# The choice of experts without GpSimd: the shift moves behind the gather, the embedding's lows move to VectorE

## Chip, cores and metric

The kernel runs on 1 core of a Trainium2 chip. The metric is the device time of one execution in microseconds (us), the median of several runs.

## The reference

Two transformer blocks follow one another on 512 tokens of 1024 channels. The first one is what matters here: two layers, each a mixer (pooling and attention in layer 0, a state space model in layer 1) and then a mixture of experts. The second block adds, in each of its two layers, a gated projection of a per-token embedding `p`.

```python
h2 = modulate(rmsnorm(x, norm2_w[layer]), shift2, scale2)     # h * (1 + scale) + shift
ffn = hier_moe(h2, ...)
x = x + gate2[:, None, :] * ffn

def hier_moe(h, w_group, b_group, w_expert, b_expert, w1, w3, w2):
    g_prob = softmax(tf @ w_group + b_group)          # 4 groups, one is taken
    g_val, g_idx = lax.top_k(g_prob, 1)
    e_logits = einsum('td,dge->tge', tf, w_expert) + b_expert
    e_val, e_idx = lax.top_k(softmax(e_logits of that group), 2)   # 2 of its 8 experts
    ...
    hid = silu(t @ w1[e]) * (t @ w3[e])               # 32 experts of width 128
    y = sum over the two experts of weight * (hid @ w2[e])

# second block, each of two layers
x = x + sigmoid(rms_norm(x) @ ple_w_gate[i]) * (p[i] @ ple_w_proj[i])
```

All of it is computed to the accuracy of float32.

## The kernel before

The five engines are TensorE (PE, products into PSUM), VectorE (DVE), ScalarE (ACT), GpSimd (POOL) and SyncE (SP, which issues DMAs). Activations lie as eight tiles of 128 channels by 512 tokens (`xs`). To keep accuracy a large product is made of three: each operand is split into a `hi` in a rounded format (a copy on ACT) and a `lo`, the difference (a subtraction, the "low"); `split` (L220) does this, `wload` (L236) loads weights and splits them, and `lin` (L253) issues the three products L268, L269 and L270 for each 128 channels.

The place of the change is the passage between a layer's mixer and its experts, in `moe` (L721), once for each of the two layers:

- `moe_begin` and its `feed` bring the router's logits: for each of the eight channel tiles an ACT copy with the scale (L715) and a product with the router's weights (L717), issued among the mixer's last projections.
- `sumsq` (L372) and `newton` (L324 to L331) make the norm's rate of each token; `lT` and the product with `fold` (L750) turn the logits so that tokens lie on partitions; L768 and L770 complete them.
- `row(i)` makes the normed rows of 128 tokens, tokens on partitions: products of `xs` with the diagonal matrix `diag` of scales (L761), built by POOL at L736, copied from PSUM by ACT with the rate (L763); POOL adds `shift` (L764), a row spread over the partitions by products with the identity (L741) and two ACT copies (L743); SP stores the rows in DRAM, `srows` (L765).
- Some 24 short DVE operations choose group and experts (L780 to L811); `both` (L811) marks both experts of each token. PE counts (`cn` L815, `rp` L817 and L820), DVE turns counts into places (L823 to L834), masks `P` and `Q` (L859 to L868) give, by products (L876), for each place the token that stands there (`at`, L878). With it POOL issues eight indirect DMAs (L966) that fetch `srows` sorted by expert; PE turns each tile of 128 rows into channels (L972), and ACT and DVE copy them from PSUM to `hT` (L975, L977), halves of 512 columns each.
- The experts follow one by one: `begin(e)` loads 3 weight tiles of 512 KB and splits `hT`'s window (L928, L929), `halves` splits weights, `product` (L947), `gate`, `turned` and `second` do the rest.

The passage leaves PE free, so an independent piece of the second block is put there: `ple_proj` (L678), a generator that projects the embedding `p` of one layer in eight pieces of six products. Its input and first four weight tiles are split with the low on POOL (`eng=G`), its later weights with the low on DVE. `step(fill, 3)` issues three pieces ahead of the index products L876, `drain(fill)` the other five behind them; results go to DRAM (L695 by SP, L991 by POOL).

What sets the order: each engine runs its own list in order. A scheduler that works with estimated times makes these lists from the program, except for PE within `tc.manual_schedule`, where the written order holds. `tc.issue_after(x)` keeps an instruction behind `x` in that order; `ready` (the copy `lT`) and the entries of `later` are such marks. Buffers come from pools: `"w"` has 3 buffers, `"we"` 4, `"wh"` and `"wl"` 2 each, PSUM tags `"pa"` and `"pm"` 2 each.

Of the kernel before, what the change touches and what calls it, by code (L numbers as in the profile page):

```python
# [140 lines left out]
def _build(ctx, tc, A, out, dbg, upto, cap):  # L141
# [78 lines left out]
    def split(src, hi, lo, scale=None, eng=V):  # L220

        if scale is None:
            S.activation(hi, src, AF.Copy)  # L223
            eng.tensor_tensor(lo, src, hi.bitcast(F32), op=SUB)  # L224
        else:
            S.activation(hi, src, AF.Copy, scale=scale)
            return V.scalar_tensor_tensor(lo, src, scale, hi.bitcast(F32), op0=MUL, op1=SUB)
# [246 lines left out]
    def mod(l, seg, c):  # L474
        return mods[l][:, seg * 8 + c:seg * 8 + c + 1]
# [202 lines left out]
    def ple_proj(l, p, done, after, later):  # L678

        hi = tl(p, [128, 1024], "wh", 1, F32R)  # L680
        lo = tl(p, [128, 1024], "wl", 1, F32R)
        w = tl(wp, [128, 1024], "w", 3)
        nc.sync.dma_start(w.rearrange("p (k t) -> p k t", k=2), A["p"][l])
        with tc.issue_after(after):
            split(w, hi, lo, eng=G)
        acts = [(hi[:, k * T:(k + 1) * T], lo[:, k * T:(k + 1) * T]) for k in range(2)]
        for n in range(8):
            if n % 4 == 0:
                with tc.issue_after(later[0] if n else after):
                    wh, wl = wload(A[f"w_pp{l}"][n:n + 4].rearrange("n p k -> p n k"), 1024, 4, eng=V if n else G)  # L690
            first.append((wh[:, n % 4 * 256:(n % 4 + 1) * 256], wl[:, n % 4 * 256:(n % 4 + 1) * 256]))
            t = f_()
            S.activation(t, lin(A[f"w_pp{l}"][n], acts), AF.Copy, scale=0.5)
            if n < 4:
                nc.sync.dma_start(pp_d[l, n], t)  # L695
            else:
                done.append(t)
            yield
# [22 lines left out]
    def moe(l, mp, lp, br):  # L721
        with ExitStack() as st:
# [8 lines left out]
            hr = [hr[:, i * 1024:(i + 1) * 1024] for i in range(9)]  # L731
            yr = [yT[t // 4].rearrange("p c t -> p (c t)")[:, t % 4 * 1024:(t % 4 + 1) * 1024] for t in range(8)]

            diag, shift = hr[4].rearrange("p (c f) -> p c f", c=8), hr[5]
            o = slice(32, 40)
            G.tensor_tensor(diag, ident[:, None, :].to_broadcast([128, 8, 128]),  # L736
                            mods[l][:, o, None].to_broadcast([128, 8, 128]), op=MUL)
            for q in range(2):
                p = ps_("pa", 2)
                for c in range(4):  # L740
                    PE.matmul(p[:, c * 128:(c + 1) * 128], mod(l, 3, 4 * q + c).to_broadcast([128, 128]), ident,  # L741
                              start=True, stop=True)
                S.activation(shift[:, q * 512:(q + 1) * 512], p, AF.Copy)  # L743
            rate = rstd_of(sumsq(xs))

            lT = tl(ep, [128, T], "lT")
# [10 lines left out]
            def row(i):  # L757
                for q in range(2):
                    p = ps_("pm" if q else "pa", 2)
                    for c in range(4):  # L760
                        PE.matmul(p[:, c * 128:(c + 1) * 128], xs[4 * q + c][:, i * 128:(i + 1) * 128], diag[:, 4 * q + c],  # L761
                                  start=True, stop=True)
                    S.activation(hr[i][:, q * 512:(q + 1) * 512], p, AF.Copy, scale=rate[:, i:i + 1])  # L763
                G.tensor_tensor(hr[i], hr[i], shift, op=ADD)  # L764
                nc.sync.dma_start(srows[i * 128:(i + 1) * 128], hr[i])  # L765

            lg = tl(ep, [128, 4, 36], "lg")
# [2 lines left out]
            V.tensor_tensor(lg, lg, br[:, None, :].to_broadcast([128, 4, 36]), op=ADD)  # L770
            for i in range(4):
                row(i)

            def b3(a, n):
                return a[:, :, None].to_broadcast([128, 4, n])
# [32 lines left out]
                                o[:, :, None, :].to_broadcast([128, 4, 4, 8]), op=MUL)  # L808
                oh.append(e)
            both = tl(ep, [128, 4, 32], "both")  # L810
            V.tensor_tensor(both, oh[0], oh[1], op=ADD)  # L811

            cn = ps_("pa", 2)
            for i in range(4):
# [149 lines left out]
            for t in range(8):  # L964
                g = yr[t]
                last = G.indirect_dma_start(out=g, out_offset=None, in_=srows,  # L966
                                            in_offset=bass.IndirectOffsetOnAxis(ap=at[:, t:t + 1], axis=0),
                                            bounds_check=511, oob_is_err=False)
                for q in range(2):
                    p = ps_("pm" if q else "pa", 2)  # L970
                    for c in range(4):
                        PE.transpose(p[:, c * 128:(c + 1) * 128], g[:, (4 * q + c) * 128:(4 * q + c + 1) * 128], ident)  # L972
                    o, pv = hT[:, 4 * q:4 * q + 4, t * 128:(t + 1) * 128], p.rearrange("p (c f) -> p c f", c=4)
                    if q:
                        S.activation(o, pv, AF.Copy)  # L975
                    else:
                        V.tensor_copy(o, pv)  # L977
                if t == 3:
                    parts = [halves(w) for w in ws[:2]]
                if t == 0:  # L980
                    ws, v, hh, hl_ = begin(0, ws)
                if t == 7:
                    hp = ps_()
                    for n in range(2):
                        product(hp, n, hh, hl_, parts[n])
                    hd, mul = gate(hp)
                if t == 7:
                    second(ws[2], turned(hd), v)
# [1136 lines left out]
```

## Time and profile before

| what | us |
|---|---|
| median of 3 runs | 2476.03 |
| lowest and highest | 2470.3, 2476.96 |
| the profiled execution, its own time | 2467.97 |
| its span, first to last instruction | 2466.2 |
| PE busy | 2339.5 (95%) |
| DVE busy | 1764.8 (72%) |
| ACT busy | 1090.6 (44%) |
| POOL busy | 518.4 (21%) |

A matmul row counts as busy while its columns stream through the array, with a modelled end, so rows overlap by a little; a float32 product is two passes and counts twice. "PEclk" is the granted clock as a share of 2.4 GHz; the chip grants 1.2 or 2.4 GHz. An idle time stands in brackets with the instruction that ended it.

### The profile page before, as it was taken

The page shows a single profiled execution, that of the slowest core. Times are in us where ns is not written, and L with a number is a line of the kernel's source. Part 1 is how long each engine was busy: PE and PEld are TensorE (multiplying, and loading weights), DVE is VectorE, ACT ScalarE, POOL GpSimd, SP SyncE. Part 2 cuts the span into 40 slices and gives each one's busy share as a digit, 9 for nine tenths or more (in the row PEclk, how much of TensorE's full clock was granted, in tenths as well). Part 3 has the DMA queues.
Part 4 walks back from the last instruction along what each step waited for, and adds up shares of the span by engine and source line. Part 5 has one row for each costly group of instructions (what it writes and reads, how often), then busy time and mean ns, then how long its engine had stood idle before and what let it go on. Part 6 is the DMA issues. An engine that isn't in the chain of part 4 may idle for free.

```text
span 2466.2 us, 35818 instructions
## 1 busy us (share of the span) xinstructions
PE 2339.5 (95%) x13205; PEld 1921.3 (78%) x13206; DVE 1764.8 (72%) x3319; ACT 1090.6 (44%) x1706; POOL 518.4 (21%) x510
## 2 busy tenths in 40 slices
PE   7999899899999998999989999999999899999999
PEld 4767799677777775899766777778787788888887
DVE  6985678699996886667686677737847756745755
ACT  3444588434443434786334434324433234433432
POOL 0001444100000002444110295666520000000000
PEclk9999899899999998999899999999999899999999
DMA  9862699554345222897421233344337632323342
GB/s 347 291 207 82 234 324 331 170 181 128 117 140 180 86 70 100 295 329 251 138 69 61 83 105 119 102 132 123 98 113 239 204 111 94 100 86 106 97 125 94
DMA packets 136790, 385.95 MB, mean 156 GB/s; under 512 B 24696, under 2 KB 41208, under 8 KB 134560
## 3 DMA queue, kind: packets, MB, share of 16 engines
q1 hardware_dynamic: 121408, 338.51, 41.5%
q0 software_dynamic: 7552, 26.74, 3.1%
q10 hardware_dynamic: 7648, 18.32, 2.1%
q8 instruction: 109, 1.79, 0.3%
q14 instruction: 73, 0.60, 0.1%
HBM read 354.13 MB, written 29.38 MB: 156 GB/s over the span
## 4 chain that ended last, share of the span: by engine, by line
PE 43%; DVE 7%; ACT 1%; issue 1%; DMA 0%; ACTq 0%; DVEq 0%
PE ps L268 13%; PE ps L270 13%; PE ps L269 13%; DVE wl L224 1%; DVE hc L2013 1%; ACT wh L223 0%; DMA tab<-tab_d 0%; PE pm L372 0%; PE sk L1587 0%; PE pa L512 0%; PE pm L530 0%; PE ps L1091 0%; PE ps L1092 0%; PE po L538 0%; DVE hc L2017 0%
## 5 line engine op out<-in xcount | busy, mean ns | idle before, releaser
L268 PE MATMUL ps<-hi,wh 128*128 128x512 f32 (+2 forms) x2248 | 898.9, 400 | 3.9 <-ACT hi L485 3.2
L270 PE MATMUL ps<-hi,wl 128*128 128x512 f32 (+2 forms) x2248 | 884.6, 394 | 8.8 <-DVE wl L224 8.8
L269 PE MATMUL ps<-lo,wh 128*128 128x512 f32 (+2 forms) x2248 | 884.5, 394 | 3.1 <-DVE lo L486 2.4
L223 ACT ACTIVATE wh<-w 128x1024 fp32r<-128x1024 f32 (+2 forms) x327 | 310.8, 951 | 572.1 <-PE ps L269 376.6
L224 DVE TENSOR_TENSOR wl<-w,wh 128x1024 fp32r<-128x1024 f32 (+3 forms) x323 | 371.3, 1150 | 211.6 <-ACT wh L223 207.3
L270 PEld LDWEIGHTS ps<-hi,wl 128*128 128x128 f32 (+1 forms) x2248 | 424.4, 189 | 109.2 <-DVE wl L224 13.8
L268 PEld LDWEIGHTS ps<-hi,wh 128*128 128x128 f32 (+1 forms) x2248 | 425.5, 189 | 106.7 <-issue 12.4
L269 PEld LDWEIGHTS ps<-lo,wh 128*128 128x128 f32 (+1 forms) x2248 | 425.2, 189 | 96.2 <-DVE lo L486 4.3
L224 DVE TENSOR_TENSOR wl<-we,wh 128x1024 fp32r<-128x1024 f32 x128 | 169.4, 1336 | 61.1 <-ACT wh L223 59.1
L929 POOL TENSOR_TENSOR hl<-hT,hh 128x1024 fp32r<-128x1024 f32 x60 | 138.4, 2307 | 173.3 <-ACT hh L928 96.0
L2013 DVE SCALAR_TENSOR_TENSOR hc<-f,cols,hc 128x511 f32<-128x511 f32 (+1 forms) x176 | 152.4, 866 | 6.4 <-ACT hc L2011 3.2
L223 ACT ACTIVATE wh<-we 128x1024 fp32r<-128x1024 f32 x128 | 135.3, 1059 | 47.6 <-PE pa L947 23.3
L909 PE MATMUL ps<-ht,w 128*128 128x128 f32 x1024 | 125.9, 276 | 5.2 <-ACT ht L959 5.0
L909 PEld LDWEIGHTS ps<-ht,w 128*128 128x128 f32 x1024 | 119.4, 192 | 7.4 <-ACT ht L959 7.1
L726 POOL IOTA io<- 128x512 f32 x2 | 1.1, 562 | 572.0 <-PE ps L270 415.6
L2009 DVE TENSOR_TENSOR f<-ps,rb 128x512 f32<-128x512 f32 x88 | 60.4, 686 | 71.2 <-PE ps L270 70.9
L441 DVE CUSTOM_DVE_ANT_0 we<-we,crow 128x1024 f32<-128x1024 f32 x80 | 96.3, 1214 | 3.4 <-DMA we<-in_ada_t_dram 3.1
L947 PE MATMUL pa<-wh,hh 128*128 128x256 f32 x496 | 89.2, 301 | 0.0
L223 ACT ACTIVATE hi<-hc 128x512 fp32r<-128x512 f32 x44 | 27.8, 632 | 128.0 <-DVE hc L2017 128.0
L491 DVE SCALAR_TENSOR_TENSOR x<-ps,mod,x 128x512 f32<-128x512 f32 x52 | 38.9, 748 | 59.0 <-PE ps L270 51.5
L947 PE MATMUL pa<-wl,hh 128*128 128x256 f32 x496 | 78.7, 281 | 1.4 <-DVE wl L224 1.4
L947 PE MATMUL pa<-wh,hl 128*128 128x256 f32 x496 | 79.1, 281 | 0.0
(572 smaller groups left out, 3319.1 us busy)
## 6 DMA issues: line engine op xcount, KB each, us to landing
we<-in_w_ex_dram SPq DMA_DIRECT2D x128, 512.0 KB, 5.7
w<-in_w_fu_dram SPq DMA_DIRECT2D x88, 512.0 KB, 3.5
we<-in_ada_t_dram SPq DMA_DIRECT2D x80, 512.0 KB, 5.0
w<-in_w_ex_dram SPq DMA_DIRECT2D x64, 512.0 KB, 5.4
w<-in_w_si_dram SPq DMA_DIRECT2D x48, 512.0 KB, 3.5
w<-in_w_fd_dram SPq DMA_DIRECT2D x32, 512.0 KB, 3.8
w<-in_w_ei_dram SPq DMA_DIRECT2D x20, 512.0 KB, 3.6
aw<-in_ada_w_dram SPq DMA_DIRECT2D x16, 512.0 KB, 10.2
```

The costliest lines, as they stand in the source:

```text
L223: S.activation(hi, src, AF.Copy)
L224: eng.tensor_tensor(lo, src, hi.bitcast(F32), op=SUB)
L268: PE.matmul(ps[:m], a, h, start=(not more and k + j == 0), stop=False)
L269: PE.matmul(ps[:m], a, l, start=False, stop=False)
L270: PE.matmul(ps[:m], b, h, start=False, stop=(last and k + j == nk - 1))
L441: V.tensor_tensor_reduce(w, w, row, 1.0, 0.0, op0=MUL, op1=ADD, accum_out=st[:, n:n + 1])
L491: V.scalar_tensor_tensor(xs[c], ps, mod(l, seg, c), xs[c], op0=MUL, op1=ADD)
L909: PE.matmul(p[:, c * 128:(c + 1) * 128], w2[:, (4 * q + c) * 128:(4 * q + c + 1) * 128], hd, start=True, stop=True)
L929: (V if e < 2 else G).tensor_tensor(hl_, win, hh.bitcast(F32), op=SUB)
L947: PE.matmul(hp[:, 0:256], h[:, 4 * n + k], w[:, k * 256:(k + 1) * 256], start=(n + i + k == 0), stop=(n + i + k == 6))
L2009: V.tensor_tensor(t, next(up)[1], rb, op=MUL)
L2013: V.scalar_tensor_tensor(c[:, d:], t[:, :T - d], C(f"fw{l}{2 - d}", n), c[:, d:], op0=MUL, op1=ADD)
```

## The change

The shift row is no longer made, and no row gets it before it is stored. It is added where the gathered and turned rows leave PSUM: there channels lie on partitions, so that the shift is one number a partition; DVE's copy becomes an addition, ACT's copy of four channel groups becomes four activations with a bias. In `ple_proj` the input and the first weights get their `hi` on ACT right behind `ready`, and their lows on DVE, behind `both` (which is now the first entry of `later`); the first part of the generator is issued by `step(fill)` ahead of the choice.

```diff
@@ ple_proj
+        wq = tl(wp, [128, 1024], "w", 3)
+        nc.sync.dma_start(wq.rearrange("p (a k) -> p a k", a=4), A[f"w_pp{l}"][0:4].rearrange("n p k -> p n k"))
+        wh, wl = (tl(wp, [128, 1024], g, 2, F32R) for g in ("wh", "wl"))
         with tc.issue_after(after):
-            split(w, hi, lo, eng=G)
+            S.activation(hi, w, AF.Copy)
+            S.activation(wh, wq, AF.Copy)
+        yield
+        with tc.issue_after(later[0]):
+            V.tensor_tensor(lo, w, hi.bitcast(F32), op=SUB)
+            V.tensor_tensor(wl, wq, wh.bitcast(F32), op=SUB)
         acts = [(hi[:, k * T:(k + 1) * T], lo[:, k * T:(k + 1) * T]) for k in range(2)]
         for n in range(8):
-            if n % 4 == 0:
-                with tc.issue_after(later[0] if n else after):
-                    wh, wl = wload(A[f"w_pp{l}"][n:n + 4].rearrange("n p k -> p n k"), 1024, 4, eng=V if n else G)
+            if n == 4:
+                with tc.issue_after(later[1]):
+                    wh, wl = wload(A[f"w_pp{l}"][n:n + 4].rearrange("n p k -> p n k"), 1024, 4)
@@ moe
-            for q in range(2):
-                p = ps_("pa", 2)
-                for c in range(4):
-                    PE.matmul(p[:, c * 128:(c + 1) * 128], mod(l, 3, 4 * q + c).to_broadcast([128, 128]), ident,
-                              start=True, stop=True)
-                S.activation(shift[:, q * 512:(q + 1) * 512], p, AF.Copy)
@@ row(i)
-                G.tensor_tensor(hr[i], hr[i], shift, op=ADD)
@@ behind the four rows
+            step(fill)
@@ both
-            V.tensor_tensor(both, oh[0], oh[1], op=ADD)
+            later.append(V.tensor_tensor(both, oh[0], oh[1], op=ADD).ins)
@@ the gathered rows
                     if q:
-                        S.activation(o, pv, AF.Copy)
+                        for c in range(4):
+                            S.activation(o[:, c], pv[:, c], AF.Identity, bias=mod(l, 3, 4 + c))
                     else:
-                        V.tensor_copy(o, pv)
+                        V.tensor_tensor(o, pv, mods[l][:, 24:28, None].to_broadcast([128, 4, 128]), op=ADD)
```

How the lists of instructions move, at three places. The first is PE's list in layer 0, from the logits' column of the seventh channel tile to the fold; `f` is a scaled channel tile, `acc` the summed squares of seven tiles, and in the second L372 row `f` the squares of the eighth. Before:

```order
L717 MATMUL pm<-f,wr 64x512
L741 MATMUL pa<-ident,mod_127 128x128 x6
L717 MATMUL pm<-f,wr 64x512
L741 MATMUL pa<-ident,mod_127 128x128 x2
L372 MATMUL pm<-ones,acc 128x1 x4
L761 MATMUL pa<-hT,x_71 128x128
L761 MATMUL pa<-hT,x_73 128x128
L372 MATMUL pm<-ones,f 128x1 x4
L750 MATMUL pm<-fold,lT 128x36 x4
```

Now:

```order
L725 MATMUL pm<-f,wr 64x512
L372 MATMUL pm<-ones,acc 128x1 x4
L763 MATMUL pa<-hT,x_71 128x128
L372 MATMUL pm<-ones,f 128x1 x4
L763 MATMUL pa<-hT,x_73 128x128
L763 MATMUL pa<-hT,x_75 128x128
L725 MATMUL pm<-f,wr 64x512
L763 MATMUL pa<-hT,x_77 128x128
L752 MATMUL pm<-fold,lT 128x36 x4
```

The products of the shift row are gone, and both products of the sums of squares stand ahead of the last logits' column instead of behind it.

The second is DVE's list in layer 0 behind `both`. Before:

```order
L811 TENSOR_TENSOR both<-oh_2280,oh_2282 128x128 [waits DVE_49]
L849 SCALAR_TENSOR_TENSOR gs<-e2m,gs 128x4 [waits DVE_49,Activation_49]
L850 RECIPROCAL wt<-gs 128x4 [waits DVE_49]
L823 SCALAR_TENSOR_TENSOR off<-ones,pa 128x32 [waits PE_49]
L851 TENSOR_TENSOR wt<-wt,e2m 128x4 [waits DVE_49]
L824 TENSOR_TENSOR off<-off,pa 128x32 [waits DVE_49]
L840 TENSOR_REDUCE most<-pa 1x1
L838 TENSOR_SCALAR ow<-off 1x32 [waits DVE_49]
L826 TENSOR_TENSOR pl<-pa,off 128x128 [waits PE_49]
```

Now:

```order
L813 TENSOR_TENSOR both<-oh_2274,oh_2276 128x128 [waits DVE_49]
L692 TENSOR_TENSOR wl<-w,wh 128x1024 [waits DMAHW1_49]
L825 SCALAR_TENSOR_TENSOR off<-ones,pa 128x32 [waits PE_49]
L693 TENSOR_TENSOR wl<-w,wh 128x1024 [waits DMAHW2_49]
L826 TENSOR_TENSOR off<-off,pa 128x32 [waits DVE_49]
L842 TENSOR_REDUCE most<-pa 1x1
L828 TENSOR_TENSOR pl<-pa,off 128x128 [waits DVE_49,PE_49]
```

Two operations of 1024 elements a partition stand on either side of the scan of the counts (`off`, the row that waits for PE), and the three short ones on the experts' weights have moved further back.

The third is ACT's list in layer 0 at the last gathered tile. Before:

```order
L975 ACTIVATE hT<-pm 128x4x128 [waits PE_49] x4
L919 TENSOR_LOAD ow [waits DVE_49]
L928 ISA
L928 ACTIVATE hh<-hT 128x1024 [waits DVE_49,Activation_49]
L223 ACTIVATE wh<-we 128x1024 [waits PE_49]
L952 ACT_TABLE_LOAD
```

Now:

```order
L978 ACTIVATE hT<-pm,mod_127 128x128 [waits PE_49]
L978 ACTIVATE hT<-pm,mod_127 128x128 x3
L223 ACTIVATE wh<-we 128x1024 [waits PE_49]
L921 TENSOR_LOAD ow [waits DVE_49]
L930 ISA
L930 ACTIVATE hh<-hT 128x1024 [waits DVE_49,Activation_49]
L954 ACT_TABLE_LOAD
```

Each half tile is four activations instead of one, and a weight copy stands ahead of the second expert's activations `hh` instead of behind them; DVE's list changes in the same way. On SP's list one expert weight of the two that stood ahead of the stores of the rows (L765) now stands right behind them, the other behind two stores of `ple_proj`'s results.

## Rows read from the trace of the kernel before

**Rows 1.** Timeline of PE, both layers (start us, length us, instruction [idle before <- releaser]).

```profile
229.27 1.60 PE L741 MATMUL pa<-ident,mod 128*128 128x128 f32 x12
...
242.99 1.06 PE L761 MATMUL pm<-hT,x 128*128 128x128 f32 x8
...
252.02 1.89 PE L815 MATMUL pa<-both,ones 128*128 128x32 f32 x8 [6.19 <-DVE both L811]
...
977.09 1.89 PE L815 MATMUL pa<-both,ones 128*128 128x32 f32 x8 [10.53 <-DVE both L811]
```

**Rows 2.** Stretches: us, busy PE, PEld, DVE, ACT, POOL; PEclk, DMA share, GB/s.

```profile
236.00:241.00 5.00, 3.50 (x19) 3.31 (x17) 4.55 (x12) 0.27 (x1) 2.84 (x2) 0.70 0.53 140
...
255.40:259.40 4.00, 4.00 (x11) 3.15 (x11) 3.64 (x19) 0.60 (x1) 0.00 (x0) 0.50 0.21 83
...
272.00:287.00 15.00, 9.97 (x71) 9.14 (x71) 8.91 (x12) 6.55 (x11) 4.73 (x7) 0.89 0.89 355
```

**Rows 3.** Timeline of DVE, layer 0.

```profile
234.88 1.68 DVE L324 TENSOR_SCALAR rsi<-rsv 128x4 int32<-128x4 int32 x1
236.59 2.27 DVE L326 TENSOR_SCALAR rsy<-rsi 128x4 int32<-128x4 int32 x1
...
240.74 0.31 DVE L768 TENSOR_TENSOR lg<-pm,rsy 128x144 f32<-128x144 f32 x1
...
242.32 2.15 DVE L787 TENSOR_TENSOR go<-go,gk 128x16 f32<-128x16 f32 x1
244.50 2.39 DVE L795 TENSOR_TENSOR el<-lg,go 128x128 f32<-128x128 f32 x1
...
247.55 1.59 DVE L782 TENSOR_TENSOR e1o<-eg,e1m 128x32 f32<-128x32 f32 x1
```

**Rows 4.** Timeline of POOL, layer 0.

```profile
228.43 1.90 POOL L736 TENSOR_TENSOR hT<-ident,mod 128x1024 f32<-128x1024 f32 x1 [70.06 <-PE ps L270]
234.17 4.67 POOL L224 TENSOR_TENSOR wl<-w,wh 128x1024 fp32r<-128x1024 f32 x2 [3.85 <-ACT wh L223]
242.07 7.02 POOL L764 TENSOR_TENSOR hT<-hT 128x1024 f32<-128x1024 f32 x3 [3.23 <-ACT hT L763]
```

**Rows 5.** Timeline of DVE, layer 1: first and last of six long operations.

```profile
957.37 0.17 DVE L324 TENSOR_SCALAR rsi<-rsv 128x4 int32<-128x4 int32 x1
...
960.62 2.04 DVE L770 TENSOR_TENSOR lg<-lg,br 128x144 f32<-128x144 f32 x1
...
972.62 1.58 DVE L782 TENSOR_TENSOR e1o<-eg,e1m 128x32 f32<-128x32 f32 x1
```

**Rows 6.** Timeline of POOL: the first gather of layer 0 and of layer 1.

```profile
263.87 1.25 POOL L966 DMA_INDIRECT yT<-srows,at  x1 [3.24 <-DVE af L880]
...
988.26 1.05 POOL L966 DMA_INDIRECT yT<-srows,at  x1 [2.57 <-DVE af L880]
```

**Rows 7.** Timeline of PE: the first expert's first product in either layer.

```profile
286.07 1.03 PE L947 MATMUL ps<-wh,hh 128*128 128x256 f32 x4
...
1008.29 0.71 PE L947 MATMUL ps<-wh,hh 128*128 128x256 f32 x4
```

**Rows 8.** Timeline of DVE, layer 0: the offsets, and the low behind the masks.

```profile
255.65 0.29 DVE L826 TENSOR_TENSOR pl<-pa,off 128x128 f32<-128x128 f32 x1 [0.79 <-PE pa L820]
...
259.25 1.22 DVE L224 TENSOR_TENSOR wl<-w,wh 128x1024 fp32r<-128x1024 f32 x1
```

**Rows 9.** Timeline of PE, layer 0: first of 30 embedding products, and what follows them.

```profile
263.22 0.48 PE L268 MATMUL ps<-wh 128*128 128x512 f32 x1
...
270.30 1.85 PE L886 MATMUL pm<-Qw,hh 128*128 128x8 f32 x16
```

**Rows 10.** Copies from PSUM: two rows of ACT's timeline, one group of the page.

```profile
286.45 0.60 ACT L975 ACTIVATE hT<-pm 128x512 f32<-128x512 f32 x1 [1.11 <-PE pm L972]
...
291.61 0.27 ACT L959 ACTIVATE ht<-pm 128x128 f32<-128x128 f32 x1
...
L2009 DVE TENSOR_TENSOR f<-ps,rb 128x512 f32<-128x512 f32 x88 | 60.4, 686 | 71.2 <-PE ps L270 70.9
```

More of the change, by code (lines that the diff above doesn't have):

```diff
@@ L732, in moe @@
             yr = [yT[t // 4].rearrange("p c t -> p (c t)")[:, t % 4 * 1024:(t % 4 + 1) * 1024] for t in range(8)]
-            diag, shift = hr[4].rearrange("p (c f) -> p c f", c=8), hr[5]
+            diag = hr[4].rearrange("p (c f) -> p c f", c=8)
             o = slice(32, 40)
```

## The prediction

> **What bounds the kernel now.** TensorE (PE) is busy nearly all of the span, so time can be won only where it stands still or runs at its lower clock. I looked at the busy slices of the page first, then at tables of stretches and the timelines by engine, for the two places the diff touches: the choice of experts in layer 0 (about 229 to 291 us) and in layer 1 (953 to 1013 us). All times below are moments of that trace. Three things are to be seen.
>
> First, PE waits for VectorE (DVE). The counts of the tokens per expert (L815) start after 6.19 us of idle in layer 0 and 10.53 us in layer 1, both times released by `both` [rows 1]. Behind the wait PE stands at half clock: the granted clock is 0.50, that is 1.2 GHz instead of 2.4, while the first embedding products run [rows 2].
>
> Second, DVE is late because of GpSimd (POOL). Operations on 4 to 128 elements a partition last 1.59 to 2.39 us where their like last 0.16 to 0.31 [rows 3]. Each of the long ones ends within 0.15 us of the end of a POOL instruction: POOL runs two lows (L224) from 234.17 and three shift additions (L764) from 242.07, about 2.34 us each, so their ends fall at 236.5, 238.8, 244.4, 246.8 and 249.1 [rows 4]; L324 ends at 236.56, L326 at 238.86, L787 at 244.47, L795 at 246.89, L782 at 249.14. The same L324 takes 0.17 us in layer 1, where POOL starts its lows later; there L770, further on, takes 2.04 [rows 5]. So the excess is a wait for POOL, not work.
>
> Third, the stage behind, in which eight gathers fetch the rows and PE turns them, is set by transfers: from 272 to 287 us PE works 10 of 15 us and the DMA engines are busy 0.89 of the time at 355 GB/s [rows 2]. It starts with the first gather, at 263.87 and 988.26 [rows 6], and ends with the first expert's product, at 286.07 and 1008.29 [rows 7]: 22.2 and 20.0 us.
>
> **What the change does, part by part.**
>
> *POOL's six instructions of each layer go* (four shift additions, two lows). With them go the excesses. Layer 0, against 0.17, 0.17, 0.17, 0.30 and 0.19 us for their like: L324 1.51, L326 2.10, L787 1.98, L795 2.09, L782 1.40; 3.6 before the logits (L768), 5.5 behind them [rows 3]. Layer 1: six such operations from L770 to L782 of `e1o`, by the same subtraction 11.1 us, all behind the logits [rows 5]. From the logits (L768, in layer 1 just ahead of L770, at 960.27) to the release of the counts the chain then takes 252.02 - 240.74 - 5.5 = 5.8 us in layer 0 and 977.09 - 960.27 - 11.1 = 5.7 in layer 1.
>
> *The eight small products that made the shift row (L741) go, with their two copies on ACT.* In layer 0 they stood between the sums of squares and the last logit column: 1.60 us for twelve passes [rows 1], four more behind it. The order now has the sums ahead of that column. From the end of the last projection at 229.27: sums 0.8 us, one row product that waits for `diag` (L736 on POOL, done at 230.33 [rows 4]), sums 0.8, so L324 could start near 231.9 instead of 234.88 and its chain, eleven short operations of 0.2 each, would end near 234.3. PE does the last column, the copy of it and the fold, and the logits start at 234.9 instead of 240.74: 5.8 us earlier, the 3.6 of above in it. In layer 1 the fold bounds them; that gives 0.5 us, and ten of the sixteen passes stood earlier among the projections: 10 x 0.11 = 1.1 us.
>
> *Where `both` is early, PE's rows end last.* The chain alone would release the counts at 240.7 and 965.5. Behind the fold PE has seven row groups of eight passes, 1.06 us with 0.17 of it under the next [rows 1]: 6.2 us, to 240.9 and 965.8. The counts start at 241.0 and 965.9 instead of 252.02 and 977.09. Layer 0 shows a granted clock of 0.70 from 236 to 241 us [rows 2], right behind many one-column products, and those stay; I charge 1.8 us for it in layer 0 alone. So the counts gain 9.2 and 11.2 us.
>
> *The lows are now two VectorE operations right behind `both`* (1.22 us each, by the second weights' low of the same shape [rows 8]), with the scan of the counts between them. Behind the start of the counts: counts 0.9 at full clock, scan 0.2, second low 1.2, two short ones 0.3; the offsets (L826) start at +2.75. From there to the end of the masks is 3.6 us before [rows 8], 0.3 more now since three short operations of the weights have moved in: +6.6. PE: its 18 products cannot pass the third before the second low, then 16 at 0.236 us (30 of them lie between 263.22 and 270.30 [rows 9]): +6.3, so they are hidden. The index products take 1.85 and the hand-over 0.5: the gathers start at +8.95 where they started at +11.85 and +11.17. That is 2.9 and 2.2 us more, and only because PE, no longer idle, keeps its full clock. If it doesn't, 16 passes of 0.21 (L815, at half clock [rows 1]) and 18 products of up to twice 0.236 make it up to +14.2: a loss of 2.4 and 3.0.
>
> The Trainium skill, page Perfetto Trace Analysis, section Optimizing Scalar/DVE Operations, speaks against this part: where VectorE is saturated, move some of its work to ScalarE or even GpSimd. By that alone the sum would lose the four lows, 4.9 us, and win nothing, as in the slower rival below. The section goes on that the two share a read port of SBUF, so that moving work between them might not help; the trace sides with that half, since VectorE's long operations end with GpSimd's.
>
> *The shift is added when turned rows leave PSUM.* On DVE a copy becomes an addition of the same 128x512, 0.69 us by a like one (L2009) [rows 10]; the copies overlap the gathers: nothing. On ACT one copy of 0.60 becomes four of 128x128, between 0.6 in all and 4 x 0.27 = 1.1 [rows 10]; I take 1.1. Eight times that is 8.6 us in a stage of 20 to 22: hidden. Only the last tile's lies open: +0.5.
>
> *Behind it* the order has a weight copy and its low (1.05 and 1.2 us) ahead of the second expert's activations, where they stood behind. With +0.5 and +1.05 on ACT and 1.2 on DVE the second expert's activations come up to 2.8 us later, while PE has the first one's 24 products to do. Bounds of PE's wait: 0 and 2.8. I take the middle, 1.3 a layer.
>
> *SP's queue.* The buffers of the lows come free later, so two expert weights that were loaded ahead of the rows' stores now stand behind them, the second behind two stores of products. By my times it lands just before the gathers; if not, it delays them by 0.5 MB at 355 GB/s, 1.5 us. I take 0, and 1.5 into the range.
>
> **Sum.** Layer 0: 9.2 + 2.9 - 1.3 = 10.8. Layer 1: 11.2 + 1.1 + 2.2 - 1.3 = 13.2. Together 24.0 us. The profiled execution took 2467.97 us (span 2466.2), so 2444; the median of the runs shown stands 8 us higher, at 2476.0, which makes 2452.
>
> **The rivals.**
> - *Half clock.* PE's stretch of short products puts it at 1.2 GHz for the rows or the products of both layers. Rows then take about 6 us longer, or the products lose 5 us, as above. Some 6 us a layer instead of the charged 1.8 in one: 24 - 10 = 14, so 2462. For: 0.70 and 0.50 were granted here. Against: the long idle ahead of the counts goes.
> - *The gathers take it back.* If weights loads meet the gathers in both layers (1.5 each) and the second expert waits the full 2.8, 6 us go: 2458.
> - *Hidden anyway.* If the stream of expert weights set the experts' end by itself, an earlier start would be given back and only a little of the sum would stay, about 2474. Against: the stream's loads start when products free their buffers, so they move with PE.
> - *Slower.* The long operations are VectorE's own and not POOL's; then nothing shrinks, the four lows lie on its chain, and the second expert waits: 4 x 1.22 + 2 x 1.4 = 7.7, so 2484. It decides as soon as the excess stays above the lows, 2.4 us a layer. Against: the ends that coincide.
>
> **How the numbers follow.** Forecast 0.62, half clock 0.17, gathers 0.12, hidden 0.06, slower 0.03. The range runs from no charge for clock and second expert (24 + 1.8 + 2.6, and some us of scatter: 2444) to half clock with the gathers' loss (14 - 5 = 9: 2466). About 0.3% (7.4 us) is what a measurement can tell from no change: faster 0.88 (forecast, clock, gathers, less a little), same 0.08, slower 0.04.
>
> **What would show it.** DVE's operations between the sums and `both` all under 0.4 us; PE's idle ahead of the counts under 2 us; granted clock 1.00 over the first products; first gather 10 to 14 us earlier relative to the last projection; the stretch from gather to first product unchanged at 20 to 22 us. I am wrong if long operations remain, if the clock stays at 0.50, or if that last stretch grows by several us.

## The result, and the profile after

| | before | changed |
|---|---|---|
| median, us | 2475.84 (2470.30 to 2476.96) | 2451.95 (2448.66 to 2458.73) |
| ratio, with its 95% interval | 1 | 0.9895 (0.9875 to 0.9915) |
| the profiled execution: its time, and its span | 2467.97, 2466.2 | 2448.66, 2446.9 |
| granted clock, mean over the span | 0.973 | 0.979 |

The change makes the kernel faster, by 1.05% on the ratio and by 23.9 us, or 0.96%, between the medians in the table. The forecast was 2452.0. The two profiled executions lie closer together, 19.3 us apart by time and by span. Two more series of the changed kernel, each beside the kernel before on the same chip, gave 0.9862 (0.9845 to 0.9879) and 0.9890 (0.9867 to 0.9913), so the gain lies between 24 and 34 us by series. What follows are the places that the prediction spoke of. Line numbers of the changed kernel stand one to three above those of the kernel before, and eight above them between `ple_proj` and the place where the shift row was made (L717 is now L725).

DVE in layer 0, timeline of the changed kernel, in answer to [rows 3] and [rows 8]:

```profile
232.62 0.17 DVE L324 TENSOR_SCALAR rsi<-rsv 128x4 int32<-128x4 int32 x1
...
235.74 0.31 DVE L769 TENSOR_TENSOR lg<-pm,rsy 128x144 f32<-128x144 f32 x1 [0.99 <-PE pm L752]
...
237.32 0.17 DVE L789 TENSOR_TENSOR go<-go,gk 128x16 f32<-128x16 f32 x1
237.53 0.29 DVE L797 TENSOR_TENSOR el<-lg,go 128x128 f32<-128x128 f32 x1
...
241.37 1.22 DVE L692 TENSOR_TENSOR wl<-w,wh 128x1024 fp32r<-128x1024 f32 x1
```

The operations that took 1.59 to 2.39 us in layer 0 take 0.17 to 0.29. The wait that is left in this chain is one for PE's fold (0.99). The first low follows behind the sum of the masks.

PE, timeline of the changed kernel, in answer to [rows 1] and [rows 7]:

```profile
228.96 1.07 PE L725 MATMUL pm<-f,wr 128*64 128x512 f32 x2
...
240.98 1.06 PE L763 MATMUL pm<-hT,x 128*128 128x128 f32 x8
241.87 0.98 PE L817 MATMUL pa<-both,ones 128*128 128x32 f32 x8
...
271.80 0.71 PE L949 MATMUL ps<-wh,hh 128*128 128x256 f32 x4
...
275.35 0.74 PE L949 MATMUL pa<-wh,hh 128*128 128x256 f32 x4 [0.53 <-ACT hh L930]
276.80 0.74 PE L949 MATMUL pa<-wh,hl 128*128 128x256 f32 x4 [0.71 <-DVE hl L931]
...
940.40 1.07 PE L725 MATMUL pm<-f,wr 128*64 128x512 f32 x2
...
944.94 1.97 PE L725 MATMUL pm<-f,wr 128*64 128x512 f32 x2
...
954.84 0.98 PE L817 MATMUL pa<-both,ones 128*128 128x32 f32 x8
...
983.82 0.72 PE L949 MATMUL ps<-wh,hh 128*128 128x256 f32 x4
...
988.80 0.74 PE L949 MATMUL pa<-wh,hl 128*128 128x256 f32 x4 [0.71 <-DVE hl L931]
```

The counts (L817) follow the last row group without idle time in both layers, where 6.19 and 10.53 us stood. They take 0.98 us instead of 1.89: PE has its full clock. Two smaller waits are new, ahead of the second expert. In layer 1 the last logits' column (944.94) takes 1.97 us instead of 1.07; the granted clock of its stretch is in the next table.

Stretches of the changed kernel (us, busy time of PE, PEld, DVE, ACT, POOL; PEclk, DMA share, GB/s), in answer to [rows 2]:

```profile
240.00:250.00 10.00, 10.00 (x70) 8.82 (x69) 8.83 (x37) 4.75 (x10) 1.21 (x1) 1.00 0.82 283
...
260.00:271.80 11.80, 6.93 (x53) 5.51 (x53) 8.50 (x12) 8.78 (x29) 3.25 (x5) 1.00 0.90 363
941.00:946.00 5.00, 4.89 (x26) 3.40 (x24) 2.10 (x13) 1.24 (x2) 1.51 (x1) 0.76 0.00 0
```

Over the counts and the first products PE is busy all of the time at full clock. In the gather stage the DMA engines are still busy 0.90 of the time at 363 GB/s, and PE only 6.93 of 11.80 us. The trace now puts most of PE's waits there down to the evictions by ACT and DVE, 4.0 us in layer 0, so that the transfers alone set the stage isn't shown; it did not get longer. The clock was lost in another place: 0.76 over layer 1's logits.

POOL, timeline of the changed kernel: the first gathers, in answer to [rows 6].

```profile
250.46 1.25 POOL L968 DMA_INDIRECT yT<-srows,at  x1 [1.03 <-DVE af L882]
...
963.41 1.05 POOL L968 DMA_INDIRECT yT<-srows,at  x1 [1.01 <-DVE af L882]
```

They start 13.41 and 24.85 us earlier than before. By layer 1's second expert (its `hl` product, 1011.64 before, 988.80 now) the changed kernel leads by 22.8 us, close to the sum of 24.0; the choice of both layers lies ahead of that point. At the end of the span the lead is 19.3 us.

### The profile page after: what moved, and what is told of

Its sections match the earlier page's. It is cut to its first block, busy times and chain, and to the rows that moved or that the text cites. A ratio compares the mean times of both kernels' runs of the same rounds, so it can differ in the third digit from the quotient of the medians.

```text
span 2446.9 us, 35789 instructions
## 1 busy us (share of the span) xinstructions
PE 2328.9 (95%) x13173; PEld 1906.3 (78%) x13174; DVE 1750.3 (72%) x3323; ACT 1096.4 (45%) x1750; POOL 486.6 (20%) x498
## 4 chain that ended last, share of the span: by engine, by line
PE 43%; DVE 7%; ACT 1%; issue 1%; DMA 0%; SPq 0%; POOL 0%; ACTq 0%; DVEq 0%; POOLq 0%
PE ps L268 13%; PE ps L270 13%; PE ps L269 13%; DVE wl L224 2%; DVE hc L2016 1%; ACT wh L223 1%; PE pm L372 0%; PE sk L1590 0%; PE pa L512 0%; DMA w<-w_d 0%; PE pm L530 0%; PE py L1715 0%; PE po L538 0%; DVE hc L2020 0%; PE pm L1580 0%
## 5 line engine op out<-in xcount | busy, mean ns | idle before, releaser
L223 ACT ACTIVATE wh<-w 128x1024 fp32r<-128x1024 f32 (+3 forms) x323 | 306.9, 950 | 572.9 <-PE ps L269 384.6
L911 PE MATMUL ps<-ht,w 128*128 128x128 f32 x1024 | 125.7, 276 | 5.1 <-ACT ht L961 5.1
L911 PEld LDWEIGHTS ps<-ht,w 128*128 128x128 f32 x1024 | 119.4, 191 | 7.0 <-ACT ht L961 6.9
L949 PE MATMUL pa<-wh,hh 128*128 128x256 f32 x496 | 88.4, 300 | 1.0 <-ACT hh L930 1.0
L949 PE MATMUL pa<-wh,hl 128*128 128x256 f32 x496 | 78.8, 280 | 1.4 <-DVE hl L931 1.4
L949 PE MATMUL pa<-wl,hh 128*128 128x256 f32 x496 | 78.6, 280 | 0.0
```

Source lines behind the costliest of these rows:

```text
L911: PE.matmul(p[:, c * 128:(c + 1) * 128], w2[:, (4 * q + c) * 128:(4 * q + c + 1) * 128], hd, start=True, stop=True)
L949: PE.matmul(hp[:, 0:256], h[:, 4 * n + k], w[:, k * 256:(k + 1) * 256], start=(n + i + k == 0), stop=(n + i + k == 6))
```

## The experiments

All of them are judged by their ratio to the kernel before on the same chip. The theory was the forecast's: work on POOL makes DVE's small operations wait. Line numbers in rows are those of the kernel shown.

**1. The first lows back on POOL, the shift left behind the gather.**

```diff
             S.activation(hi, w, AF.Copy)
+            G.tensor_tensor(lo, w, hi.bitcast(F32), op=SUB)
             S.activation(wh, wq, AF.Copy)
+            G.tensor_tensor(wl, wq, wh.bitcast(F32), op=SUB)
...
-        with tc.issue_after(later[0]):
-            V.tensor_tensor(lo, w, hi.bitcast(F32), op=SUB)
-            V.tensor_tensor(wl, wq, wh.bitcast(F32), op=SUB)
```

> The embedding's first two low parts go back to GpSimd; everything else is as after the change. Theory (what GpSimd does beside VectorE stretches VectorE's long operations): one to three of the long ones of each layer come back (the logits' copy or additions at 2 us or more where the changed kernel has 0.17 to 0.3), 2 to 6 us more than after for both layers together, so 2454 to 2458 us, with no low part between the sum of the chosen (line 813) and the copy of the counts. Rival (VectorE is the one that was loaded, the lows cost it 1.2 us each on the way): this is up to 4.9 us faster than the changed kernel, 2447 to 2452 us, and the long operations stay short.

Measured: 2457.65 us, ratio 0.9918 (0.9894 to 0.9943). DVE has less to do than in the changed kernel, and the time is longer, as the theory had it (2454 to 2458). By the ratios alone that is weak, since the interval touches those of two of the changed kernel's three series (0.9895 and 0.9890); the trace is what shows it. Timelines of POOL and DVE, layer 0:

```profile
237.78 2.36 POOL L689 TENSOR_TENSOR wl<-w,wh 128x1024 fp32r<-128x1024 f32 x1 [4.58 <-ACT wh L688]
240.11 2.43 POOL L691 TENSOR_TENSOR wl<-w,wh 128x1024 fp32r<-128x1024 f32 x1
...
237.94 0.31 DVE L768 TENSOR_TENSOR lg<-pm,rsy 128x144 f32<-128x144 f32 x1 [0.99 <-PE pm L751]
238.28 2.03 DVE L770 TENSOR_TENSOR lg<-lg,br 128x144 f32<-128x144 f32 x1
240.34 0.17 DVE L781 TENSOR_REDUCE gm<-lg 128x4 f32<-128x16 f32 x1
240.55 2.02 DVE L783 TENSOR_TENSOR go<-lg,gm 128x16 f32<-128x16 f32 x1
```

POOL's lows end at 240.14 and 242.54, DVE's two long operations at 240.31 and 242.57. L768 has the same size as L770 and runs beside the same low in 0.31 us: one of its inputs is in PSUM, while both inputs of L770 are in SBUF. A reduction (one input) isn't held either. The counts then wait 3.13 us in layer 0 and 2.93 in layer 1, where the changed kernel has no wait. The theory holds; the rival, that the lows weigh on DVE, would have made this kernel the faster one. The advice weighed in the prediction, that moving work of a saturated VectorE to ScalarE or even GpSimd may make sense (the Trainium skill, page Perfetto Trace Analysis, section Optimizing Scalar/DVE Operations), wins nothing here, 0.9918 against the changed kernel's 0.9862 to 0.9895; the section's own doubt, that it might not help because the two share a read port, fits what this run's rows show.

**2. The shift back ahead of the stores, the lows left on DVE.** The row's products, its copies and POOL's four additions come back, with plain evictions behind the gather (the change's own lines in `moe`, undone).

> The shift row, its TensorE products and GpSimd's four additions per layer come back ahead of the stores of rows; the embedding's lows stay on VectorE. Theory (GpSimd's work stretches VectorE's): most of the change's gain goes, 12 to 18 us for both layers, so 2464 to 2470 us; the one-hot or threshold operations of layer 0 take 1.5 us or more again, and TensorE idles several us ahead of the count products. Rival (the order of TensorE's work alone, the shift's products ahead of the logits): 3 to 5 us more than after, 2455 to 2457 us, with the small VectorE operations at 0.2 to 0.3 us.

Measured: 2466.97 us, ratio 0.9951 (0.9934 to 0.9968), as the theory had it. By the ratios the shift alone would give about 0.8% (run 1) and the lows alone 0.5% (this run), 20 and 12 us of that chip's 2480. Timelines of POOL, DVE and PE, layer 0:

```profile
249.84 2.35 POOL L772 TENSOR_TENSOR hT<-hT 128x1024 f32<-128x1024 f32 x1 [2.66 <-ACT hT L771]
...
249.89 3.38 DVE L692 TENSOR_TENSOR wl<-w,wh 128x1024 fp32r<-128x1024 f32 x1
...
250.12 1.88 PE L824 MATMUL pa<-both,ones 128*128 128x32 f32 x8 [6.08 <-DVE both L820]
```

And a stretch of it:

```profile
250.00:255.00 5.00, 4.88 (x19) 4.27 (x20) 4.99 (x8) 0.00 (x0) 2.19 (x1) 0.50 0.26 105
```

DVE's low, 1.22 us long in the changed kernel, takes 3.38. It begins 0.05 us behind a POOL addition of 2.35 us, and what is left of that addition and 1.22 us of its own make up the 3.38 to within 0.15. PE's wait ahead of the counts is back, and behind it the granted clock of 0.50.

**3. POOL works, but nothing waits for it.** Four additions on POOL per layer whose result nobody reads; rows are stored as in the changed kernel, and PE's list is the changed kernel's.

```diff
                     S.activation(hr[i][:, q * 512:(q + 1) * 512], p, AF.Copy, scale=rate[:, i:i + 1])
+                G.tensor_tensor(hr[5], hr[i], hr[4], op=ADD)
                 nc.sync.dma_start(srows[i * 128:(i + 1) * 128], hr[i])
```

> The changed kernel with one more GpSimd addition behind each of the four gathered-row blocks of each layer (it reads two tiles in SBUF and writes one that nobody uses); no wait is added for any other engine. Theory: VectorE's small two-input operations that fall beside them take 1.5 us or more, TensorE runs out of fill ahead of the counts, and the time is 5 to 15 us above the changed kernel's, 2457 to 2467 us. Rival (GpSimd's additions cost only because the rows' stores waited for them): the time stays at 2450 to 2454 us.

Measured: 2468.72 us, ratio 0.9957 (0.9938 to 0.9976), 1.7 us above the expected stretch. POOL's and DVE's timelines, layer 0, and PE's:

```profile
239.30 9.62 POOL L766 TENSOR_TENSOR hT<-hT 128x1024 f32<-128x1024 f32 x4 [6.75 <-ACT hT L765]
...
240.03 1.66 DVE L785 TENSOR_TENSOR e1o<-eg,e1m 128x32 f32<-128x32 f32 x1
241.73 2.40 DVE L787 TENSOR_TENSOR e1o<-e1o,desc 128x32 f32<-128x32 f32 x1
244.16 0.19 DVE L789 TENSOR_REDUCE e1k<-e1o 128x4 f32<-128x32 f32 x1
244.39 2.17 DVE L790 TENSOR_TENSOR e1o<-e1o,e1k 128x32 f32<-128x32 f32 x1
246.59 2.38 DVE L804 SCALAR_TENSOR_TENSOR e<-e1o,eg 128x32 f32<-128x32 f32 x1
...
250.99 1.89 PE L818 MATMUL pa<-both,ones 128*128 128x32 f32 x8 [7.42 <-DVE both L814]
```

This is the cleanest of the runs. No engine waits for the additions' result, and still four operations of 32 elements a partition take 1.7 to 2.4 us, the counts wait 7.42 us (7.02 in layer 1), and about as much is lost as when the shift itself comes back (0.9957 against 0.9951). So the cost comes without any store that waits for POOL; the rival had put it there.

**4. POOL writes, but doesn't read.** Eight fills of a tile by POOL behind the diagonal. In layer 0 they run from 231.60 to 239.61 us, beside the rate, the logits and the choice of the group; run 3's additions came later, beside the choice of the experts (239.30 to 248.92).

```diff
+            for _ in range(8):
+                G.memset(hr[5], 0.0)
```

> The changed kernel with eight GpSimd fills of a tile (128x1024, write only) per layer behind the diagonal. If only GpSimd work that reads SBUF stretches VectorE's two-input operations, the logits' additions and one-hots stay at 0.17 to 0.5 us and the time within 2 us of the changed kernel, 2450 to 2454 us; the copies and threshold operations alone may stretch. If any GpSimd work does it, it looks like the run with additions: operations of 1.5 us or more and 2457 to 2467 us.

Measured: 2450.65 us, ratio 0.9880 (0.9852 to 0.9908), the changed kernel's. POOL's and DVE's timelines, layer 0:

```profile
231.60 8.01 POOL L747 MEMSET hT<- 128x1024 f32 x8
...
233.27 0.32 DVE L324 TENSOR_SCALAR rsi<-rsv 128x4 int32<-128x4 int32 x1
233.62 0.97 DVE L326 TENSOR_SCALAR rsy<-rsi 128x4 int32<-128x4 int32 x1
...
238.31 0.31 DVE L773 TENSOR_TENSOR lg<-lg,br 128x144 f32<-128x144 f32 x1
...
238.85 0.17 DVE L786 TENSOR_TENSOR go<-lg,gm 128x16 f32<-128x16 f32 x1
```

POOL is busy for 8 us, and of DVE's operations in that time only the two integer ones of the tensor-scalar form are held, until the fill then under way ends (8.01 us for eight, so about 1 us each). The two-input operations L773 and L786 keep their 0.31 and 0.17 us; beside the lows of run 1 the same two (L770 and L783 there) took 2.03 and 2.02. So two kinds of waiting stood in [rows 3]: L324 and L326 waited beside the lows there and wait beside the fills here, the two-input ones waited only beside POOL work that reads SBUF. The time of this run says less, since its fills lie elsewhere than run 3's additions.

The Trainium skill, page SBUF — State Buffer, section Who interferes with whom, gives this as its rule: DVE's second pair of SBUF ports is GpSimd's as well and is held by one of them for a whole instruction; a DVE operation with two inputs in SBUF collides with GpSimd instructions that read SBUF and not with those that only write, reductions never collide, and forms such as the tensor-scalar one can take the pair when they run in their fast mode. The waits of runs 1, 3 and 4 agree with each of these points, with the rows above; the ports themselves are in no row, and that L324 and L326 ran in such a mode is not shown by one either.

**5. The tail: is the new wait ahead of the second expert worth anything?** The second half of expert 1's weights is split behind that expert's `hh` and `hl` instead of ahead of them, in ACT's and DVE's lists. In run 6 the last gathered tile is also evicted by DVE alone.

```diff
-                    parts.append(halves(ws[1]))
+                    if e == 1:
+                        with tc.issue_after(behind[0]), tc.issue_after(behind[1]):
+                            parts.append(halves(ws[1]))
+                    else:
+                        parts.append(halves(ws[1]))
```

> The changed kernel itself, as the reference on this chip for the three that follow: 2446 to 2459 us, as in its first runs, and a ratio to before of 0.987 to 0.992.

> The changed kernel with the second half of expert 1's weights split behind that expert's input halves (lines 930 and 931) on ScalarE and VectorE, instead of ahead of them. Theory (the tail's 1.3 us per layer is this queue): TensorE's two waits ahead of the second expert (0.53 and 0.71 us in layer 0, 0.49 and 0.71 in layer 1) fall to 0.3 us in all or less, and the time is 1 to 2.5 us below the changed kernel's of the same chip. Rival (the gate of the first expert, now behind that split on ScalarE, is waited for instead): the waits move to the turned gate (line 959 there) and the time stays within 1 us.

> As the run before it, and the last gathered tile's second half is also evicted by VectorE in one addition instead of ScalarE's four. Theory: the input half (line 930) starts some 0.4 us earlier than in the run before, the first expert's product is not later, and the time is 0 to 1 us below that run's. Rival: VectorE's second addition (0.69 us) comes behind its first and makes the first expert's product as late as it makes the second's input early: no difference.

Measured: 2451.67 and 2451.75 us, ratios 0.9897 (0.9881 to 0.9912) and 0.9890 (0.9874 to 0.9906); the changed kernel beside them on the same chip had 2443.73 and 0.9862 (0.9845 to 0.9879), which is itself just below what was expected of it. Both runs miss their gain. Timeline of PE in run 5, layer 0:

```profile
280.55 0.74 PE L951 MATMUL pa<-wh,hl 128*128 128x256 f32 x4 [0.58 <-DVE hl L931]
283.80 2.05 PE L911 MATMUL ps<-ht,w 128*128 128x128 f32 x16 [0.51 <-ACT ht L963]
288.85 0.74 PE L951 MATMUL pa<-wl,hh 128*128 128x256 f32 x4 [0.56 <-DVE wl L224]
```

The wait for `hh` is gone and the second expert's `hl` product starts 4.12 us behind the first expert's first product instead of 5.00. Behind it PE waits for the first expert's turned gate (0.51), as the rival had it, and further on for a low of the weights (0.56). But the changed kernel has waits of its own there, so the balance has to be read at equal work: the third group of L911, behind the same 96 matmuls of L951 (L949 there), starts in layer 0 17.72 us behind the first expert's first product in run 5 and 17.57 in run 6, against 17.93 to 18.12 in the changed kernel's three profiles; in layer 1 it is 17.75 and 18.00 against 17.95 to 18.10. What the new order wins at that place is half a us a layer or less, too little for these runs to tell, and the rival's "within 1 us" didn't come true either: the medians lie 8 us above the one beside them. Whether the two are really slower than the changed kernel stays open: run 5's interval lies above that one's by a hair, run 6's overlaps it, and both cover the changed kernel's other two ratios. No version here is faster than the changed kernel.

**7. Only the shift row's products taken out of the kernel before.** POOL's additions stay and add another tile.

```diff
-            for q in range(2):
-                p = ps_("pa", 2)
...
-                S.activation(shift[:, q * 512:(q + 1) * 512], p, AF.Copy)
```

> The kernel before without the shift row's sixteen products and its two evictions; GpSimd's four additions stay and add another tile, so the rows lack their right shift. Theory (GpSimd's work is the main cost, the products' place a small one): 2 to 4 us below the kernel before, VectorE's long operations stay (four or more of 1.5 us and over in layer 0), and TensorE still idles 4 us or more ahead of the counts. Rival (the products ahead of the logits' last projection carry much of the gain): 8 us or more below before.

Measured: 2480.07 us, ratio 1.0009 (0.9998 to 1.0021): nothing. PE's order ahead of the logits is now nearly the changed kernel's, POOL is as before, and so is the wait; timeline of PE, layers 0 and 1:

```profile
255.09 1.89 PE L809 MATMUL pa<-both,ones 128*128 128x32 f32 x8 [7.13 <-DVE both L805]
...
982.11 1.88 PE L809 MATMUL pa<-both,ones 128*128 128x32 f32 x8 [10.55 <-DVE both L805]
```

Even the 2 to 4 us that the theory gave the products didn't come. But with POOL as before the counts wait for `both`, so this run can't say what the products cost where PE's rows end last; run 8 can.

**8. The products put back into the changed kernel,** with their two copies, into a tile that nothing reads, so that PE's list is the one of before and POOL is quiet. They are eight products, sixteen passes, in each layer.

```diff
+            for q in range(2):
+                p = ps_("pa", 2)
+                for c in range(4):
+                    PE.matmul(p[:, c * 128:(c + 1) * 128], mod(l, 3, 4 * q + c).to_broadcast([128, 128]), ident,
+                              start=True, stop=True)
+                S.activation(shift[:, q * 512:(q + 1) * 512], p, AF.Copy)
```

> The changed kernel itself, beside the run that follows on the same chip: 2443 to 2459 us, a ratio to before of 0.984 to 0.992.

> The changed kernel with the shift row's sixteen products and two evictions put back in their place ahead of the logits, into a tile that nothing reads; GpSimd adds nothing and the shift stays behind the gather, so the result is whole. It prices TensorE's order alone, with GpSimd quiet. Theory (the forecast's terms: about 1.8 us of products per layer that stand ahead of the logits, and the ten or so products of rows that no longer stand there): 2 to 5 us above the changed kernel for both layers, VectorE's operations all at 0.2 to 0.3 us, no idle time of TensorE ahead of the counts over 1 us. Rival (the products fill time in which TensorE waits for the row sums anyway, as taking them out of the kernel before changed nothing): within 1.5 us of the changed kernel.

Measured: 2447.97 us, ratio 0.9884 (0.9861 to 0.9908); the changed kernel beside it 2448.33, ratio 0.9890 (0.9867 to 0.9913). The medians are 0.4 us apart, within the scatter of either kernel's runs: the rival's case by its number, though not by its reason. The first and last rows of run 8's PE timeline, from the seventh logits' column of layer 0 to the counts:

```profile
229.84 1.07 PE L725 MATMUL pm<-f,wr 128*64 128x512 f32 x2
...
244.53 1.05 PE L823 MATMUL pa<-both,ones 128*128 128x32 f32 x8 [0.62 <-DVE both L819]
```

That is 14.69 us, where the changed kernel's first profile has 12.91 (228.96 to 241.87), both at full clock: the products cost 1.8 us there. In layer 1 it is 13.36 us, against 12.92 in runs 4 and 6 and 12.93 in run 5, which have the changed kernel's order up to there and kept their clock. Stretches of the changed kernel of this series, both layers:

```profile
235.00:240.00 5.00, 5.00 (x31) 3.63 (x30) 2.43 (x14) 3.73 (x6) 0.00 (x0) 0.80 0.00 0
...
946.00:951.00 5.00, 5.00 (x23) 4.75 (x23) 2.36 (x11) 3.51 (x5) 0.00 (x0) 0.50 0.00 2
```

And of run 8:

```profile
235.00:240.00 5.00, 5.00 (x47) 5.00 (x47) 3.22 (x19) 3.87 (x6) 0.00 (x0) 1.00 0.00 0
...
946.00:951.00 5.00, 4.73 (x32) 3.61 (x32) 2.12 (x13) 2.21 (x4) 0.00 (x0) 1.00 0.01 2
```

In its profile the changed kernel loses its clock over the last logits and the first rows, for part of the stretch in layer 0 and for all of it in layer 1; run 8 keeps 2.4 GHz throughout. In these two executions the balance comes out even: the seventh column of layer 1 starts 4.0 us later in run 8 (943.79 against 939.77), the counts at the same moment (957.15 against 957.17).

That the products keep the clock up isn't shown. The kernel before has them, in the order of run 8, and lost its clock in layer 0 all the same (0.70 in [rows 2]); the changed kernel's first profile hasn't and kept it there. Over all the profiles at hand the clock fell in this stretch in one of six passages with the products and in nine of eighteen without them. That fits the idea and proves nothing; what decides where it falls stays open.

## Why the prediction was right

Point by point, against the steps of the prediction. Gains are read against the seventh logits' column of the same layer (L717, now L725), so that what happened ahead of it drops out. Its rows in the kernel before, and there the second expert's `hl` product in each layer:

```profile
228.27 1.07 PE L717 MATMUL pm<-f,wr 128*64 128x512 f32 x2
...
289.74 0.68 PE L947 MATMUL pa<-wh,hl 128*128 128x256 f32 x4
...
953.04 1.07 PE L717 MATMUL pm<-f,wr 128*64 128x512 f32 x2
...
1011.64 0.68 PE L947 MATMUL pa<-wh,hl 128*128 128x256 f32 x4
```

- *POOL's excess, 9.1 and 11.1 us, goes.* Right, and now shown: runs 1 and 3 bring long operations back by POOL work that reads SBUF, in run 3 by work that nothing else waits for; run 4 doesn't bring the two-input ones back by work that only writes.
- *PE's rows end last.* Right. Allowing for the 0.69 us by which everything starts later in this execution (the seventh tile's logits' column: 228.27 before, 228.96 now), the counts of layer 0 were to start at 241.7 without the charge for the clock; they start at 241.87.
- *Half clock, 1.8 us in layer 0 alone.* About the right size, in the wrong layer, and not a fixed place at all. In the profiled execution layer 0 kept its clock and the counts gained 10.84 us instead of 9.2; layer 1 lost it, and they gained 9.6 instead of 11.2. The changed kernel's profiles of the other two series lost it in layer 1 (column to counts 17.40 us) and in both layers (14.14 and 17.40). So the loss is between nothing and 4.5 us a layer, and the prediction, which tied it to the one-column products, had no way to say where. The rival of half clock in both layers is what the third series' profile shows (0.80 and 0.50), yet that execution has the same span, 2447.0 us, and the merging of layer 1's experts begins at the same moment (its first transposition, L1054, at 1145.02 us, 1144.92 in the first profile), though its counts were 2.3 us later. As a loss of 10 us it didn't come.
- *L741's products, 2.2 us in layer 0 beside POOL's 3.6, and 1.6 in layer 1.* The time is there where the clock is full: the logits start 8.87 us behind the column in run 8 (238.71, on DVE) and 6.78 in the changed kernel's first profile (235.74), a difference of 2.1. But the total shows none of it; runs 7 and 8 leave the medians where they were. In the profiles without the products the loss of clock, 1.2 to 4.5 us where it falls, is as large as what they save, and the prediction charged it once.
- *Counts to gathers, +8.95 us.* Measured +8.59 and +8.57, so 3.3 and 2.6 us were won instead of 2.9 and 2.2. Against the column the first gathers come 14.1 and 12.2 us earlier, where 10 to 14 was named as the sign.
- *The gather stage unchanged, 20 to 22 us.* 21.3 and 20.4 us from the first gather to the first expert's product. Whatever ACT's four activations a tile and DVE's addition cost, they don't lengthen it.
- *The tail, 1.3 us a layer.* From the first expert's first product to the second's `hl` product 3.67 us became 5.00, and 3.35 became 4.98: 1.3 and 1.6. But it doesn't last. The kernel before has its own waits a little further on (0.91 us for a low in layer 0), and the third group of L909 (now L911) starts 17.86 and 17.91 us behind the first product before, 18.11 and 18.10 now: by then only 0.2 us a layer is lost.
- *SP's queue at nothing.* It fits the unchanged gather stage; not tried by itself.
- *Hidden anyway,* and *slower:* neither. Layer 0's lead reaches layer 1, and run 1, with fewer VectorE operations, is slower than the changed kernel.

The sum was 24.0 us, and 22.8 are there at layer 1's second expert, but its two halves were off in opposite ways. Against the column, layer 0 gained 13.6 us at its second expert's `hl` product instead of 10.8: no loss of clock (1.8), a gather stage 0.9 shorter. Layer 1 gained 10.2 instead of 13.2: the clock (1.6), the ten passes among its projections, which show nowhere (1.1; the lead is 15.4 us at the first product that merges layer 0's experts, L1091 before and L1094 now, and 12.6 at layer 1's column), and a tail and a gather stage each some tenths longer. Behind layer 1's experts the lead of the two profiled executions moves between 17 and 26 us, where the code is the same, and ends at 19.3; no run here explains that. The forecast took the sum off the profiled execution (2444, measured 2448.66) and added the distance to the median. That the median then came out within 0.1 us is luck: the errors of the halves cancel, and the same kernel's gain was 27 and 34 us in the other two series. What is right is the mechanism and the size of its main terms. One slip doesn't matter for this: half clock with the gathers' loss, 14 - 5 = 9, gives 2467 and not 2466 for the end of the range.

## What to carry to other kernels

A VectorE operation that is ten times as long as its like, and whose end coincides with the end of a GpSimd instruction, was waiting here and not working: look at what GpSimd reads then, and price the removal by the excess, not by GpSimd's own time. GpSimd that only fills tiles was a better neighbour here than GpSimd that adds, and giving GpSimd a share of the work beside a chain of small two-input VectorE operations can cost more than it saves. Before crediting saved TensorE products in a sparse stretch, look at the granted clock in several executions: here eight unused products a layer cost up to 1.8 us at equal clock and nothing that the medians show.

## What the runs showed that was not expected

The wait is paid whole by the small operation, shown as its own busy time and not as idle time: 2.40 us for 32 elements a partition (run 3) against 0.19. And the kind of POOL work matters: 9.6 us of additions a layer cost some 15 to 24 us in all (0.9957 against the changed kernel's 0.9895, 0.9890 and 0.9862, of 2476), while 8 us of fills a layer, in an earlier place, cost nothing that shows (0.9880, 0.9852 to 0.9908).
